# Order of the first projections, how queries and keys are turned, the instruction order of the first stage, and the PSUM banks of a hybrid encoder step

## The chip, the cores and the metric

The kernel runs on one core of a Trainium2 chip. The metric is the device time of one execution in microseconds. One execution is taken by the hardware profiler; its trace gives, for each engine, when each instruction started, how long it took and what it waited for. TensorE (PE) multiplies matrices into PSUM, a memory of eight banks; VectorE (DVE) and ScalarE (ACT) read PSUM and work elementwise; GpSimd (POOL) does small elementwise work; SyncE (SP) issues nearly all transfers (DMAs).

## What is computed

One layer of a streaming encoder, for 256 prompt frames and 8 streams of 16 new frames each: 384 rows (three blocks of 128) of width 2048.

```python
h = rmsnorm(x, norm_mix_g)
proj = h @ w_in                      # columns: GLU pair | q | k | v | forget logits | gate A | gate B
u = glu_in[..., :D_CONV] * sigmoid(glu_in[..., D_CONV:])
z = layernorm(causal_dwconv(concat(conv_buf, u), conv_dw_w, conv_dw_b), conv_ln_g, conv_ln_b)
a_out = (z * sigmoid(z)) @ conv_pw_out
q, k = rmsnorm(q, q_norm_g), rmsnorm(k, k_norm_g)        # per head of 128
logf = log_sigmoid(f_logit + b_forget)
b_out = attn(q, k, v, logf) @ w_att_out                  # 8 heads, bias = cumulative logf, causal
x = x + (gate_a * a_out + gate_b * b_out) @ w_out
up = rmsnorm(x, norm_ffn_g) @ w_up                       # 2 x 5632 columns
x = x + (silu(causal_dwconv(g_half)) * u_half) @ w_down
```

The sample streams also attend to 128 cached keys and values each. Besides `x`, the new keys, values, log forget gates and convolution states are returned. All is float32.

## The kernel before

**Matmuls.** Each weight is read once. `planned` (line 155) lists the weight tiles in the order in which they are used; a unit is two 128-row blocks of one column group. `ahead` (199) fetches units by `fetch` (132, SP's queue, three buffers `raw`) and calls `split` (148): ScalarE copies the unit into a rounded high part `hi` (line 145) and VectorE computes the rest `lo` (146). Activations are kept as such a pair too. A product is then three matmuls (lines 244 to 246, or 239 to 241 in the transposed kind): high with high, high with low, low with high. `gemm` (221) runs a list of jobs; a job is one group of up to 512 columns over all 16 blocks of rows, with one PSUM bank for each of the three row blocks. The tiles come from two pools: `acc` with five banks and `misc` with three. All three of a job come from `acc`, but for the second job of a pair, whose third comes from `misc`. After the last block the job's `evac` moves the banks to SBUF.

**Side work.** After every block of rows (an iteration) `gemm` calls `tick`, which advances generators given to it; through them small steps are placed between matmuls. TensorE's instructions are issued in program order. On the other engines a scheduler chooses the order by priority and by its own estimate of when data will be there. Two means fix it: `tc.high_priority(offset=...)`, and `queued` (92), which chains an instruction behind the one on its engine that was queued last. Before, `queued` is used for transfers on SP alone.

**The first stage.** `x_chunk(c)` (282) turns a 128-column chunk of x on TensorE (285) and ScalarE (288) and VectorE (289) make its high and low part `hT`. Chunks 0 and 1 and the first two units are made in a prologue, the others by `first_norm` (388) during the first gemm (439): the value columns are three groups of 344 (the last one with the eight forget logits), the first two as a pair, the third alone. Chunks 2 and 3 are made in iterations 3 and 4. `first_norm` also squares x on ScalarE (400) and computes the row scale `rs1`, which the evacuations `tok_evac` (423) apply. Then come the forget logits, the value outputs (465, 466), the keys (514, with `bias_rows` beside), scaling of the keys by their norm (519, 520) and the key outputs, the queries (524) and their scaling (528).

**Attention and GLU.** The GLU projection (745) has four jobs with four banks each; its 64 iterations carry `attention` (651) and the depthwise convolution `conv` (686) as side work. Head h starts at iteration 5 + 6h: `head_past_keys` (569) turns cached keys on VectorE, `head_operands` (576) turns the head's query and key on TensorE (lines 583 and 587, three transposes each) and copies them out of PSUM (584 ScalarE, 588 VectorE), `head_scores` (592), `head_probs` (617), `head_out` (629) and `head_last` (646) follow at offsets 2, 4, 9, 11 and 13. `load_k` and `load_v` (546, 553) fetch caches and bias rows for a head, through SP.

**Later stages.** Gates (823), attention and convolution outputs (834, 874), the output projection (932) and the feed-forward part (1027) are `gemm` calls of the same kind. `blocks` (255) turns a panel of 384 x 512 by 16 VectorE transposes of 32 x 384; it is used there already (line 259). `mix_panel` (857) is such a use, and `mix_chunk` (847) turns the last panel on TensorE.

Of the kernel before, what the change touches and what calls it, by code (L numbers as in the profile page):

```python
# [19 lines left out]
H = 8  # L20
# [13 lines left out]
SPLIT_AHEAD, EVAC_AHEAD = 150, 400  # L34
# [6 lines left out]
def hybrid_step(  # L41
# [66 lines left out]
    make_identity(nc, ident[:])  # L108

    def newton_rsqrt(r, s, m):  # L110
        nc.scalar.activation(s, m, AF.Sqrt)
# [79 lines left out]
    v_last = len(plan) - 16  # L191
    ready = []
# [28 lines left out]
    def gemm(jobs, sides=()):  # L221
        for js in jobs:
            js = js if isinstance(js, tuple) else (js,)
            for j in js:
                nb = 4 if j["kind"] == "A" else NTT
                j["ps"] = [(misc_tile if j is not js[0] and i == 2 else acc_tile)() for i in range(nb)]
            for j, k in [(j, k + i) for k in range(0, js[0]["nk"], 2) for j in js for i in range(2)]:
# [19 lines left out]
                if sp:  # L247
                    with tc.high_priority(offset=EVAC_AHEAD):
                        for m in range(nb):
                            j["evac"](m, ps[m])  # L250
                    if "done" in j:
# [30 lines left out]
    def x_chunk(c):  # L282
# [5 lines left out]
        nc.scalar.activation(hi, ps[:, :NT], AF.Identity, scale=g)  # L288
        stt(lo, ps[:, :NT], g, f(hi), op0=ALU.mult, op1=ALU.subtract)  # L289
# [57 lines left out]
    for v, r, n in rows:  # L347
        nc.gpsimd.dma_start(vrow[r:r + n, :], v[0].rearrange("(c p) -> c p", p=P))
    kg = p_qkv.tile([P, P], F32, name="kg")
    nc.gpsimd.dma_start(kg[:], k_norm_g[0].partition_broadcast(P))  # L350
    bf = p_qkv.tile([P, H], F32, name="bf")
    nc.gpsimd.dma_start(bf[:], b_forget[0].partition_broadcast(P))
# [35 lines left out]
    def first_norm():  # L388
        for c in range(2, 16, 2):
# [6 lines left out]
            if c % 4 == 2:  # L396
                for t in range(NTT):
                    n = c // 4
                    tc.keep_in_program_order(
                        nc.scalar.activation(junk[:], xs[n][:, t, :], AF.Square, accum_out=ssx[:, t, n:n + 1]))  # L400
            yield
            if c > 2:
                yield
        mt = p_x0.tile([P, NTT], F32, name="mt")
        nc.vector.tensor_reduce(mt[:], ssx[:], axis=mybir.AxisListType.X, op=ALU.add)
        ts(mt[:], mt[:], 1.0 / DM, EPS, op0=ALU.mult, op1=ALU.add)
        r = rsqrt(mt[:], [P, NTT], p_x0, "r1")
        nc.vector.tensor_copy(rs1[:], r[:])
        for _ in range(12):
# [13 lines left out]
    def tok_evac(dst, c0, n, sq=None, shared=True):  # L423
        def ev(t, ps):
            if shared and t % 2:
                ts(dst[:, t, c0:c0 + n], ps[:, :n], rs1[:, t:t + 1], None, op0=ALU.mult)
            else:
                nc.scalar.activation(dst[:, t, c0:c0 + n], ps[:, :n], AF.Identity, scale=rs1[:, t:t + 1])
            if sq is not None:
                for i in range(n // P):  # L430
                    jk = p_qkv.tile([P, P], F32, tag="jk", bufs=2, name="jk")
                    h = c0 // P + i
                    nc.scalar.activation(jk[:], dst[:, t, h * P:(h + 1) * P], AF.Square,
                                         accum_out=ssq[:, sq, t, h:h + 1])
# [4 lines left out]
    gemm([(v_jobs[0], v_jobs[1]), v_jobs[2]], [first_norm()])  # L439
    close_x0()  # L440
# [23 lines left out]

    nc.sync.dma_start(prompt_v[0, 0].rearrange("(t p) h d -> p t (h d)", p=P), vt[:, 0:2, 0:1024])
    nc.sync.dma_start(sample_v[0].rearrange("b t h d -> (b t) (h d)"), vt[:, 2, 0:1024])
# [47 lines left out]
    gemm([job("B", 16, ha, tok_evac(kt, 512 * i, 512, 0)) for i in range(2)], [bias_rows()])  # L514
    close_b()
    rk = head_rsqrt(0)
# [6 lines left out]

    gemm([job("B", 16, ha, tok_evac(qt, 512 * i, 512, 1)) for i in range(2)])
    rq = head_rsqrt(1)
    for t in range(NTT):
        q3 = qt[:, t, :].rearrange("p (h d) -> p h d", h=H)
        tt(q3, q3, rq[:, t, :].unsqueeze(2).to_broadcast([P, H, P]), op=ALU.mult)
# [15 lines left out]
    kcs, vbs = {}, {}  # L544
# [8 lines left out]
    def load_v(h):  # L553
        vc = p_att.tile([P, 8, P], F32, tag="vc", bufs=2, name="vc")
        nc.sync.dma_start(vc[:], cache_v[0, :, :, h, :].rearrange("b p d -> p b d"))
        bs = p_att.tile([P, 5 * P], F32, tag="bs", bufs=2, name="bs")
# [8 lines left out]
        vbs[h] = vc, bs  # L565
# [10 lines left out]
    def head_operands(d):  # L576
        hs = d["hs"]
        d["vc"], d["bs"] = vbs[d["h"]]
        qT = p_att.tile([P, NT], F32, tag="qT", bufs=2, name="qT")
        kT = p_att.tile([P, NT], F32, tag="kT", bufs=2, name="kT")  # L580
        ps = misc_tile()
        for t in range(NTT):
            tr(ps[:, t * P:(t + 1) * P], qt[:, t, hs], ident[:])
        nc.scalar.activation(qT[:], ps[:, :NT], AF.Identity, scale=qgs[:])
        ps = misc_tile()
        for t in range(NTT):
            tr(ps[:, t * P:(t + 1) * P], kt[:, t, hs], ident[:])
        nc.vector.tensor_copy(kT[:], ps[:, :NT])
        nc.vector.tensor_copy(qz[d["h"] % 2][:, :, :, 0:16], by_stream(qT[:, 2 * P:]))
        d["qT"], d["kT"] = qT, kT  # L590

    def head_scores(d):
        qT, kT, kTs, bs, qzh = d["qT"], d["kT"], d["kTs"], d["bs"], qz[d["h"] % 2]
# [479 lines left out]
```

## Time and profile before

| | us |
|---|---|
| median of three runs | 2005.61 |
| lowest and highest run | 2002.94, 2005.78 |
| the profiled execution | 2005.83 |
| its span in the trace | 2003.9 |
| TensorE busy | 1992.6 |
| VectorE busy | 1272.2 |
| ScalarE busy | 742.1 |

The span runs from the first to the last instruction. Busy time of TensorE is modelled, since matmuls overlap in its pipeline: two matmuls that start 0.22 us apart are each shown with 0.39 us. So distances between starts tell more than durations. The granted clock is the share of TensorE's full clock, 2.4 GHz; its other level is 1.2 GHz.

### The profile page before, as it was taken

How to read it: one execution, taken by the hardware profiler on the slowest of the kernel's cores; microseconds unless marked ns; L12 is line 12 of the kernel's file. 1: busy time of each engine (PE TensorE's matmuls, PEld its weight loads, DVE VectorE, ACT ScalarE, POOL GpSimd, SP SyncE). 2: the span in 40 equal slices, each digit the busy share in tenths (PEclk: the TensorE clock that was granted, in tenths of full speed). 3: DMA queues.
4: the chain of work that ended last, by engine and by line, in shares of the span. 5: the costliest groups of instructions: out<-in, count | busy, mean ns of one | idle time of the engine just before them, and what ended most of it. 6: DMA issues, size and time to landing. Idle time of an engine off the chain costs nothing.

```text
span 2003.9 us, 24493 instructions
## 1 busy us (share of the span) xinstructions
PE 1992.6 (99%) x9431; PEld 1681.5 (84%) x9431; DVE 1272.2 (63%) x1852; ACT 742.1 (37%) x1077; POOL 87.2 (4%) x216
## 2 busy tenths in 40 slices
PE   8999999999999999999999999999999999999999
PEld 8988999988888887888888888888888888888887
DVE  4435478888765487676867683367673376638663
ACT  5434455433334523334433432233332233323321
POOL 2000001100000000000010000001000000000000
PEclk9999999999999999999999999999999999999999
DMA  6566566444444334534444444444443444344443
GB/s 179 176 175 175 137 163 167 120 140 131 132 134 125 127 121 142 185 121 133 127 137 116 137 127 137 126 127 126 129 135 127 133 120 137 126 129 125 137 157 106
DMA packets 209254, 275.99 MB, mean 138 GB/s; under 512 B 55878, under 2 KB 96729, under 8 KB 209129
## 3 DMA queue, kind: packets, MB, share of 16 engines
q1 hardware_dynamic: 208817, 273.85, 46.3%
q8 instruction: 74, 1.21, 0.2%
q0 software_dynamic: 288, 0.57, 0.2%
q14 instruction: 43, 0.35, 0.1%
q10 hardware_dynamic: 32, 0.01, 0.0%
HBM read 266.98 MB, written 7.86 MB: 137 GB/s over the span
## 4 chain that ended last, share of the span: by engine, by line
PE 95%; DVE 4%; issue 1%; DMA 1%; ACT 0%; SPq 0%; ACTq 0%; DVEq 0%
PE acc L244 28%; PE acc L246 28%; PE acc L245 28%; PE acc L239 2%; PE acc L241 2%; PE acc L240 2%; DVE mixT L259 1%; DVE lo L146 1%; DMA raw<-in_w_in_dram 1%; DVE sgA L843 0%; DVE uT L259 0%; DVE sgA L844 0%; PE misc L636 0%; PE misc L603 0%; PE misc L285 0%
## 5 line engine op out<-in xcount | busy, mean ns | idle before, releaser
L146 DVE TENSOR_TENSOR lo<-raw,hi 128x1024 fp32r<-128x1024 f32 (+2 forms) x481 | 579.6, 1205 | 582.7 <-ACT hi L145 579.0
L145 ACT CAST hi<-raw 128x1024 fp32r<-128x1024 f32 (+2 forms) x481 | 496.0, 1032 | 994.2 <-PE acc L246 869.1
L244 PE MATMUL acc<-hi,xg 128*128 128x512 f32 x1056 | 411.8, 390 | 0.0
L246 PE MATMUL acc<-hi,xg 128*128 128x512 f32 x1056 | 410.9, 389 | 0.0
L245 PE MATMUL acc<-lo,xg 128*128 128x512 f32 x1056 | 410.8, 389 | 0.0
L244 PE MATMUL acc<-hi,hT 128*128 128x512 f32 (+1 forms) x704 | 268.5, 381 | 2.4 <-ACT hT L288 2.4
L246 PE MATMUL acc<-hi,hT 128*128 128x512 f32 (+1 forms) x704 | 266.0, 378 | 0.4 <-DVE hT L289 0.4
L245 PE MATMUL acc<-lo,hT 128*128 128x512 f32 (+1 forms) x704 | 265.8, 377 | 0.0
L244 PEld LDWEIGHTS acc<-hi,xg 128*128 128x128 f32 x1056 | 198.2, 188 | 42.3
L246 PEld LDWEIGHTS acc<-hi,xg 128*128 128x128 f32 x1056 | 198.2, 188 | 41.3
L245 PEld LDWEIGHTS acc<-lo,xg 128*128 128x128 f32 x1056 | 198.2, 188 | 40.6
L244 PE MATMUL acc<-hi,act 128*128 128x512 f32 x528 | 205.5, 389 | 0.5 <-DVE y L1018 0.5
L246 PE MATMUL acc<-hi,act 128*128 128x512 f32 x528 | 205.4, 389 | 0.0
L245 PE MATMUL acc<-lo,act 128*128 128x512 f32 x528 | 205.4, 389 | 0.0
L722 DVE SCALAR_TENSOR_TENSOR ut<-ext,cw,ut 128x384 f32<-128x384 f32 x240 | 151.5, 631 | 6.1
L244 PEld LDWEIGHTS acc<-hi,hT 128*128 128x128 f32 x704 | 132.7, 189 | 25.3 <-ACT hT L288 2.7
L246 PEld LDWEIGHTS acc<-hi,hT 128*128 128x128 f32 x704 | 132.7, 189 | 23.3 <-DVE hT L289 0.7
L245 PEld LDWEIGHTS acc<-lo,hT 128*128 128x128 f32 x704 | 132.8, 189 | 22.2
L259 DVE STREAM_TRANSPOSE extf<-tok 32x384 f32<-32x384 f32 x176 | 100.3, 570 | 30.9 <-ACT tok L954 28.2
L259 DVE STREAM_TRANSPOSE uT<-tok 32x384 f32<-32x384 f32 x176 | 100.3, 570 | 29.7 <-ACT tok L954 26.9
L244 PEld LDWEIGHTS acc<-hi,act 128*128 128x128 f32 x528 | 99.1, 188 | 21.6 <-DVE y L1018 0.9
L245 PEld LDWEIGHTS acc<-lo,act 128*128 128x128 f32 x528 | 99.1, 188 | 20.5
(289 smaller groups left out, 2079.7 us busy)
## 6 DMA issues: line engine op xcount, KB each, us to landing
raw<-in_w_up_dram SPq DMA_DIRECT2D x176, 512.0 KB
raw<-in_w_in_dram SPq DMA_DIRECT2D x96, 512.0 KB
raw<-in_w_down_dram SPq DMA_DIRECT2D x88, 512.0 KB
raw<-in_w_in_dram SPq DMA_DIRECT2D x64, 256.0 KB
raw<-in_w_out_dram SPq DMA_DIRECT2D x32, 512.0 KB
raw<-in_w_att_out_dram SPq DMA_DIRECT2D x16, 512.0 KB
raw<-in_conv_pw_out_dram SPq DMA_DIRECT2D x16, 512.0 KB
raw<-in_w_in_dram SPq DMA_DIRECT2D x23, 344.0 KB
```

The costliest lines, as they stand in the source:

```text
L145: nc.scalar.copy(hi[:, k, :o], raw[:, k, :o])
L146: tt(lo[:, k, :o], raw[:, k, :o], f(hi[:, k, :o]), op=ALU.subtract)
L239: mm(o, hi[:, kk, s], ah, start=st, stop=False)
L240: mm(o, hi[:, kk, s], al, start=False, stop=False)
L241: mm(o, lo[:, kk, s], ah, start=False, stop=sp)
L244: mm(o, ah[:, s], hi[:, kk, :n], start=st, stop=False)
L245: mm(o, ah[:, s], lo[:, kk, :n], start=False, stop=False)
L246: mm(o, al[:, s], hi[:, kk, :n], start=False, stop=sp)
L259: nc.vector.transpose(put(a, slice(32 * b, 32 * b + 32)), src[32 * a:32 * a + 32, b])
L722: stt(o, v, wc, o, op0=ALU.mult, op1=ALU.add)
```

## The change

The change has four parts, and they touch the first 20% of the kernel and the choice of banks in all of it.

- **Order.** The first pair is the first and third value group; then come the queries, the keys, and the second value group alone; then the GLU as before. The value outputs move behind the second value group. `first_norm` spreads over the first gemm and the query gemm, and its pool is closed after that.
- **Queries and keys.** `q_panel` and `k_panel` turn them with `blocks` on VectorE, four heads at a time: queries during the key gemm (at iterations 2 and 12) into `attT`, which ScalarE scales in place; keys during the second value group (at 3 and 13) into the memory of the queries. `head_operands` keeps the cached keys and one small copy. Squares for the norms are issued after a job's evacuation, not within it.
- **First stage chained.** `queued` now also chains, while the first pair and four more units are fetched, the splits, the two parts of each x chunk, the last squares, the root and the ScalarE evacuations, in program order; on GpSimd the identity stands ahead of the small loads. Attention steps get a priority of 250. Bias rows are loaded apart from the cached values, which are loaded one head ahead; the last two steps of a head move by one iteration.
- **Banks.** With `wide=True` the third bank of every job comes from `misc`, so that five and three banks rotate; this is set for every gemm but the first, the second value group and the GLU.

```diff
     ident = cp.tile([P, P], F32, name="ident")
-    make_identity(nc, ident[:])
+    nc.gpsimd.memset(ident[:], 0.0)
+    queued(nc.gpsimd.affine_select(out=ident[:], in_=ident[:], pattern=[[-1, P]], compare_op=ALU.not_equal, fill=1.0,
+                                   base=0, channel_multiplier=1))
...
-        nc.scalar.copy(hi[:, k, :o], raw[:, k, :o])
-        tt(lo[:, k, :o], raw[:, k, :o], f(hi[:, k, :o]), op=ALU.subtract)
+        first = in_first()
+        queued(nc.scalar.copy(hi[:, k, :o], raw[:, k, :o]), first)
+        queued(tt(lo[:, k, :o], raw[:, k, :o], f(hi[:, k, :o]), op=ALU.subtract), first)
...
-    planned(w_in, 0, V_COLS[0], 16, V_COLS[1])
-    for cols in V_COLS[2:] + K_COLS + Q_COLS + GLU_COLS + GA_COLS + GB_COLS:
+    planned(w_in, 0, V_COLS[0], 16, V_COLS[2])
+    for cols in Q_COLS + K_COLS + V_COLS[1:2] + GLU_COLS + GA_COLS + GB_COLS:
...
+    def in_first():
+        return len(plan) >= v_last - 4
...
-                j["ps"] = [(misc_tile if j is not js[0] and i == 2 else acc_tile)() for i in range(nb)]
+                j["ps"] = [(misc_tile if i == 2 and (wide or j is not js[0]) else acc_tile)() for i in range(nb)]
...
-        nc.scalar.activation(hi, ps[:, :NT], AF.Identity, scale=g)
-        stt(lo, ps[:, :NT], g, f(hi), op0=ALU.mult, op1=ALU.subtract)
+        with tc.high_priority(offset=EVAC_AHEAD):
+            queued(nc.scalar.activation(hi, ps[:, :NT], AF.Identity, scale=g))
+            queued(stt(lo, ps[:, :NT], g, f(hi), op0=ALU.mult, op1=ALU.subtract))
...
-    gemm([(v_jobs[0], v_jobs[1]), v_jobs[2]], [first_norm()])
-    close_x0()
+    norm_steps = first_norm()
+    gemm([(v_jobs[0], v_jobs[2])], [norm_steps])
...
+    gemm([tok_job(qt, 512 * i, 512, 1) for i in range(2)], [norm_steps, bias_rows()], wide=True)
+    drain(norm_steps)
...
+    def q_panel(n):
+        blocks(qt[:, :, 512 * n:512 * (n + 1)], by_feature(attT[:, 4 * n:4 * n + 4]))
+        for h in range(4 * n, 4 * n + 4):
+            nc.scalar.activation(attT[:, h], attT[:, h], AF.Identity, scale=qgs[:])
+
+    kT = qt[:].rearrange("p t n -> p (t n)").rearrange("p (h x) -> p h x", h=H)
+
+    def k_panel(n):
+        blocks(kt[:, :, 512 * n:512 * (n + 1)], by_feature(kT[:, 4 * n:4 * n + 4]))
+
+    for n in range(2):
+        after(2 + 10 * n, lambda n=n: q_panel(n))
+    gemm([tok_job(kt, 512 * i, 512, 0) for i in range(2)], wide=True)
...
+    for n in range(2):
+        after(3 + 10 * n, lambda n=n: k_panel(n))
+    gemm([v_jobs[1]])
+    nc.sync.dma_start(prompt_v[0, 0].rearrange("(t p) h d -> p t (h d)", p=P), vt[:, 0:2, 0:1024])
+    nc.sync.dma_start(sample_v[0].rearrange("b t h d -> (b t) (h d)"), vt[:, 2, 0:1024])
...
     def head_operands(d):
-        hs = d["hs"]
-        d["vc"], d["bs"] = vbs[d["h"]]
-        qT = p_att.tile([P, NT], F32, tag="qT", bufs=2, name="qT")
-        kT = p_att.tile([P, NT], F32, tag="kT", bufs=2, name="kT")
-        ps = misc_tile()
-        for t in range(NTT):
-            tr(ps[:, t * P:(t + 1) * P], qt[:, t, hs], ident[:])
-        nc.scalar.activation(qT[:], ps[:, :NT], AF.Identity, scale=qgs[:])
-        ps = misc_tile()
-        for t in range(NTT):
-            tr(ps[:, t * P:(t + 1) * P], kt[:, t, hs], ident[:])
-        nc.vector.tensor_copy(kT[:], ps[:, :NT])
-        nc.vector.tensor_copy(qz[d["h"] % 2][:, :, :, 0:16], by_stream(qT[:, 2 * P:]))
-        d["qT"], d["kT"] = qT, kT
+        head_past_keys(d)
+        d["bs"] = bss[d["h"]]
+        nc.vector.tensor_copy(qz[d["h"] % 2][:, :, :, 0:16], by_stream(attT[:, d["h"], 2 * P:]))
...
-            for off, step in ((0, head_past_keys), (2, head_operands), (4, head_scores), (9, head_probs),
-                              (11, head_out), (13, head_last)):
+            for off, step in ((1, head_operands), (4, head_scores), (9, head_probs),
+                              (12, head_out), (14, head_last)):
```

## Rows read from the trace of the kernel before

**Rows 1.** The page's first part: busy us of each engine, share, instructions.

```profile
PE 1992.6 (99%) x9431; PEld 1681.5 (84%) x9431; DVE 1272.2 (63%) x1852; ACT 742.1 (37%) x1077; POOL 87.2 (4%) x216
```

**Rows 2.** Busy time by stretch: stretch, PE, PEld, DVE, ACT, POOL (starts); clock, DMA share, GB/s.

```profile
75.00:100.00 25.00, 25.00 (x135) 22.50 (x134) 12.10 (x28) 9.93 (x12) 0.00 (x0) 1.00 0.75 230
...
175.00:200.00 25.00, 25.00 (x112) 20.71 (x111) 8.62 (x8) 10.97 (x32) 0.00 (x0) 1.00 0.61 171
...
225.00:250.00 25.00, 25.00 (x161) 24.57 (x160) 14.74 (x31) 9.72 (x17) 0.81 (x2) 1.00 0.62 158
...
275.00:300.00 25.00, 25.00 (x191) 23.85 (x190) 24.07 (x57) 11.77 (x24) 1.16 (x2) 1.00 0.71 167
...
1700.00:1725.00 25.00, 24.52 (x108) 19.96 (x108) 20.57 (x31) 9.78 (x13) 0.00 (x0) 1.00 0.40 133
```

**Rows 3.** Timeline at 12.8 to 17.8 us: start, duration, what [idle before it <- releaser].

```profile
12.85 0.77 ACT L145 CAST hi<-raw 128x688 fp32r<-128x688 f32 x1 [3.96 <-DMA raw<-in_w_in_dram]
...
14.94 0.77 ACT L145 CAST hi<-raw 128x688 fp32r<-128x688 f32 x1 [1.32 <-DMA raw<-in_w_in_dram]
15.61 0.57 ACT L288 ACTIVATE hT<-misc,gm 128x384 fp32r<-128x384 f32 x1
...
16.23 0.43 PE L244 MATMUL acc<-hi,hT 128*128 128x344 f32 x1 [2.44 <-ACT hT L288]
...
16.53 0.61 DVE L289 SCALAR_TENSOR_TENSOR hT<-misc,gm,hT 128x384 fp32r<-128x384 f32 x1
...
17.19 0.45 PE L246 MATMUL acc<-hi,hT 128*128 128x344 f32 x1 [0.38 <-DVE hT L289]
```

**Rows 4.** Busy time by slices of 2 us behind that pause, columns as in rows 2.

```profile
16.00:18.00 2.00, 1.39 (x5) 1.11 (x6) 2.00 (x4) 1.97 (x6) 0.00 (x0) 0.86 0.64 181
18.00:20.00 2.00, 2.00 (x8) 2.00 (x8) 0.45 (x1) 1.41 (x4) 0.00 (x0) 0.50 0.95 305
20.00:22.00 2.00, 2.00 (x12) 1.98 (x12) 0.00 (x0) 0.44 (x1) 0.00 (x0) 0.78 0.68 223
```

**Rows 5.** Timeline of PE around the transposes of one head.

```profile
249.77 0.34 PE L241 MATMUL acc<-hT,lo 128*128 128x384 f32 x1
249.95 0.49 PE L583 MATMUL misc<-ident,qt 128*128 128x128 f32 x3
...
250.52 0.42 PE L239 MATMUL acc<-hT,hi 128*128 128x384 f32 x1
250.78 0.33 PE L240 MATMUL acc<-hT,hi 128*128 128x384 f32 x1
```

**Rows 6.** Groups by line and shape, DVE and ACT: busy us, mean ns of one.

```profile
L259 DVE STREAM_TRANSPOSE yT<-y 32x384 f32<-32x384 f32 x64 | 36.5, 570 | 1.2
...
L146 DVE TENSOR_TENSOR lo<-raw,hi 128x688 fp32r<-128x688 f32 x23 | 20.2, 878 | 35.2 <-ACT hi L145 35.0
...
L519 DVE TENSOR_TENSOR kt<-kt,rq0r 128x1024 f32<-128x1024 f32 x3 | 3.6, 1220 | 0.0
...
L433 ACT ACTIVATE jk<-kt 128x128 f32<-128x128 f32 x24 | 7.1, 298 | 0.1
```

**Rows 7.** Timeline of PE where a job waits for a bank or operand.

```profile
721.59 0.39 PE L246 MATMUL acc<-hi,zt 128*128 128x512 f32 x1
722.16 0.50 PE L244 MATMUL acc<-hi,zt 128*128 128x512 f32 x1 [0.18 <-DVE sgB L828]
722.50 0.40 PE L245 MATMUL acc<-lo,zt 128*128 128x512 f32 x1
...
755.32 0.50 PE L244 MATMUL acc<-hi,zt 128*128 128x512 f32 x1 [0.19 <-DVE sgB L828]
...
791.91 0.33 PE L850 MATMUL misc<-ident,sgA 128*128 128x128 f32 x1 [0.23 <-DVE sgA L844]
...
1721.80 0.39 PE L246 MATMUL acc<-hi,act 128*128 128x512 f32 x1
1722.67 0.50 PE L244 MATMUL acc<-hi,act 128*128 128x512 f32 x1 [0.48 <-DVE y L1018]
```

More of the change, by code (lines that the diff above doesn't have):

```diff
@@ L219, in tick, with gemm @@
             next(g, None)
-    def gemm(jobs, sides=()):
+    def gemm(jobs, sides=(), wide=False):
         for js in jobs:
@@ L398, in first_norm @@
                     n = c // 4
[L399 to L402, printed above, removed]
+                    sq = nc.scalar.activation(junk[:], xs[n][:, t, :], AF.Square, accum_out=ssx[:, t, n:n + 1])
+                    if c == 14:
+                        queued(sq)
+                    else:
+                        tc.keep_in_program_order(sq)
+            if c < 14:
+                yield
+            if 2 < c < 14:
                 yield
         mt = p_x0.tile([P, NTT], F32, name="mt")
[L405 to L409, printed above, removed]
+        with tc.high_priority(offset=EVAC_AHEAD):
+            nc.vector.tensor_reduce(mt[:], ssx[:], axis=mybir.AxisListType.X, op=ALU.add)
+            ts(mt[:], mt[:], 1.0 / DM, EPS, op0=ALU.mult, op1=ALU.add)
+            r = rsqrt(mt[:], [P, NTT], p_x0, "r1")
+            nc.vector.tensor_copy(rs1[:], r[:])
+        for _ in range(14):
             yield
@@ L421, in hybrid_step, with tok_job, post, tok_evac @@
     ssq = p_qkv.tile([P, 2, NTT, H], F32, name="ssq")
-    def tok_evac(dst, c0, n, sq=None, shared=True):
+    def tok_job(dst, c0, n, sq):
+        d = job("B", 16, ha, tok_evac(dst, c0, n))
+        def post():
+            for t in range(NTT):
+                for h in range(c0 // P, (c0 + n) // P):
+                    jk = p_qkv.tile([P, P], F32, tag="jk", bufs=2, name="jk")
+                    nc.scalar.activation(jk[:], dst[:, t, h * P:(h + 1) * P], AF.Square,
+                                         accum_out=ssq[:, sq, t, h:h + 1])
+        d["post"] = post
+        return d
+    def tok_evac(dst, c0, n, shared=True):
         def ev(t, ps):
@@ L427, in ev @@
             else:
[L428 to L434, printed above, removed]
+                queued(nc.scalar.activation(dst[:, t, c0:c0 + n], ps[:, :n], AF.Identity, scale=rs1[:, t:t + 1]),
+                       in_first())
         return ev
@@ L659, in attention @@
                 step, d = at[t]
-                step(d)
-                if step is head_out and d["h"] + 2 < H:
-                    load_v(d["h"] + 2)
+                with tc.high_priority(offset=ATT_AHEAD):
+                    step(d)
+                if step is head_probs and d["h"] + 2 < H:
+                    load_b(d["h"] + 2)
+                if step is head_probs and 0 < d["h"] < H - 1:
+                    load_v(d["h"] + 1)
             yield
@@ L741, in hybrid_step @@
     load_k(0)
+    load_b(0)
     load_v(0)
+    load_b(1)
     load_v(1)
@@ L822, in hybrid_step @@
     ln_steps = conv_branch()
-    gemm([job("B", 16, ha, sig_evac(sg, n)) for sg in (sgA, sgB) for n in range(4)], [ln_steps])
+    gemm([job("B", 16, ha, sig_evac(sg, n)) for sg in (sgA, sgB) for n in range(4)], [ln_steps], wide=True)
     def ao_evac(n):
@@ L832, in ao_job @@
         return job("B", 8, grouped(aHL), ao_evac(n))
-    gemm([ao_job(n) for _, n in AO_PW[:2]], [ln_steps])
+    gemm([ao_job(n) for _, n in AO_PW[:2]], [ln_steps], wide=True)
     drain(ln_steps)
@@ L874, in hybrid_step @@
     gemm([ao_job(n) if what == "ao" else job("B", 8, grouped(zt), pw_evac(n), done=pw_done(n))
-          for what, n in AO_PW[2:]])
+          for what, n in AO_PW[2:]], wide=True)
     res = {}
@@ L930, in second_norm @@
         nc.vector.tensor_copy(rs2[:], r2[:])
-    gemm([job("B", 16, grouped(mix), wo_evac(n), done=wo_done(n)) for n in range(4)])
+    gemm([job("B", 16, grouped(mix), wo_evac(n), done=wo_done(n)) for n in range(4)], wide=True)
     p_f, y, xg, rs2, close_f, close_r = (res[k] for k in ("f", "y", "xg", "rs2", "close_f", "close_r"))
@@ L1026, in hybrid_step @@
     for what, g in FFN_PLAN:
-        gemm(up_jobs(g) if what == "up" else down_jobs(g, g[-1] == 10))
+        gemm(up_jobs(g) if what == "up" else down_jobs(g, g[-1] == 10), wide=True)
     pe_order.__exit__(None, None, None)
```

41 lines of the change are left out of this document (21 added, 20 removed).

## The prediction

> **What bounds the kernel now.** I read the page's busy shares first: TensorE is busy for 99% of the span [rows 1]. A share of 99% says that the time is the sum of what TensorE is given, so an edit pays in three ways only: it takes instructions off TensorE, it ends one of TensorE's few pauses, or it avoids matmuls at the low clock. Next I read the busy times by stretch [rows 2]. In 175 to 200 us 112 full matmuls start, so one takes 25.00/112 = 0.223 us, and TensorE is full in every stretch shown but the last, even where VectorE is itself nearly full (24.07 of 25.00 us in 275 to 300) or where the 1.5 MiB of values go out (75 to 100). VectorE has 8.62 us of work in 175 to 200. Last I looked for TensorE's pauses: one at 14 us [rows 3], followed by a stretch at the lower clock [rows 4], and a few of under half a microsecond where the next accumulation waits for a bank [rows 7].
>
> **The change part by part.** The sum is made against the profiled execution, 2005.83 us for a span of 2003.9; the median of the runs, 2005.61, is 0.2 us from it, which I neglect.
>
> *Queries and keys turned by VectorE.* Before, `head_operands` turns the three 128-row blocks of a head's query and of its key on TensorE. The first of six transposes starts at 249.95, the next main matmul at 250.52, that is 0.57 us; and this matmul holds the next one off until 250.78, 0.26 us where such matmuls lie 0.18 apart (249.77 to 249.95) [rows 5]. So 0.57 + 0.08 = 0.65 us a head, and 8 heads give 5.2 us. These lie on TensorE, on the path, and go entirely. VectorE instead gets `blocks`: 16 transposes for each panel of four heads, two panels for queries and two for keys, 64 in all. The nearest row is the same form elsewhere, 0.570 us [rows 6], so 36.5 us, less the eight copies `kT<-PSUM` that fall away. They lie beside the key projection and the last value block. The first has room: the two panels of queries are 18.3 us, and the key gemm is 288 matmuls of 0.223, 64 us, in which VectorE's other work is about a third by the stretch 175 to 200. For keys the room is narrower and is the second rival. Price here: 0 as long as that cover holds. Below nothing is possible only through the small copies; I leave it at 0.
>
> *First stage chained.* The pause at 14 us: ScalarE takes the third weight unit at 12.85, when it lands, then waits for the fourth, which lands at 14.94, and only then, at 15.61, evacuates chunk 2 of x, whose transposes TensorE had finished at 13.8 (16.23 less the 2.44 that it then stood). The main matmuls resume at 16.23 and, after a second wait for VectorE's half, at 17.19 [rows 3]. In the chain the order is that of the program: the split of unit 3 is issued before the third iteration, chunk 2 and chunk 3 behind it, and unit 4 after them. So chunk 2's high half starts when the split ends, 12.85 + 0.77 = 13.62, and ends 0.57 later at 14.2; its low half follows the split's low half on VectorE (13.6 + 0.88 [rows 6] = 14.5) and ends 0.61 later, at 15.1. The third matmul can then start at 15.1 instead of 17.19: a gain of 2.05 us, which the landing at 12.85 does not let grow. Unit 4 has landed by 14.94 and is needed only an iteration pair later, near 17.7; nothing new is late behind it at once. The squares of the norm stand in that gap and might delay it by some 0.5 us.
>
> Behind the pause comes a stretch at 1.2 GHz: the granted clock is 0.86, 0.50 and 0.78 in the three slices of 2 us from 16 to 22 [rows 4], so 2 x (0.14 + 0.50 + 0.22) = 1.7 us of full-clock work are lost. Whether this goes too is not shown: the new pauses, about 0.4 us at 13.8 and 0.6 before the third matmul, lie between one of 2.44 us that was followed by the low clock [rows 3] and one of 0.48 us that was not (clock 1.00 in 1700 to 1725 [rows 2, 7]). Bounds 0 and 1.7; they are nearer to the short one in size, so I take 1.7. The identity made ahead of the small loads starts the warm-up earlier, but the third unit's landing at 12.85 sets what follows, so I count at most 0.2 us and take 0.
>
> The chain also puts the last squares, the root and the splits in one line on ScalarE. Evacuations of the first value block need that root. It was ready in time before, with the same work ahead of it and only one wider split now between, so I take 0; bound 1 us of loss.
>
> *Order of the blocks.* The matmuls of values, queries and keys are the same in number and width; only their order changes, so 0 on TensorE. What moves with them: the two output DMAs of the values (1.5 MiB), from the stretch 75 to 100 to behind the last value block, at about 215 us, past the caches' loads on SP's queue; the key outputs, also 1.5 MiB, are issued during that block. Behind them on SP stand weight loads. The cover is the three raw buffers and three split ones; the third rival is that it is gone. The later value cache loads (at the step before use, not two heads ahead) have 9 iterations of 12 matmuls, about 19 us, before they are read: 0.
>
> *Eight banks.* `wide` puts the third accumulation of each job into the other pool, so a job no longer waits for the one before it to be evacuated. At 722 the start-to-start distance is 0.57 us and the next one, 0.34, is 0.11 over the pitch, so 0.57 - 0.23 + 0.11 = 0.46; a second such wait is at 755; at 1722 it is 0.87 - 0.23 + 0.11 = 0.75 [rows 7]. Together 1.7 us. A fourth of this kind, at the first job of the output projection, I count at 0: at 791.91 TensorE waits anyway for VectorE's `sgA`, and VectorE does not get there sooner. The pool keeps one or two banks for the small transposes, where a wait may appear; with the boundary from the last value block, whose three evacuations are all ScalarE's, I take 0.5 us of loss, with bounds 0 and 2.
>
> Sum: 5.2 + 2.05 + 1.7 + 1.7 - 0.5 = 10.15 us, so 2005.8 - 10.15 = 1995.7.
>
> **The rivals.** *The pause keeps its clock, or more.* The low clock stays after the shorter pauses: 1.7 us less, 1997.4. If the third unit's transfer and not ScalarE's order holds the stage, so that the chain does not do what it says, its 3.75 us go altogether: 1999.4. Against that speaks that the transposes were done at 13.8 and only ScalarE stood between.
>
> *VectorE becomes the bound between the values and the gates.* From the start of the last value block the keys need 12 squares on ScalarE, 0.30 us each with a read behind each, 4 to 7 us in all, then the root and six multiplications of 1.22 us, 32 transposes of 0.57 and the splits, 0.88 each [rows 6]: with the root the first panel is ready at about 8 + 7.3 + 9.1 and 8 for nine splits, 32 us, both at about 32 + 9.1 and another 8 for splits and evacuations, 50. The first scores stand at the tenth iteration of the gate stage, about 16 x 9 matmuls of 344 columns, 0.15 us each by the pitch of 512, and 9 iterations of 12 x 0.18: 21.6 + 19.4 = 41 us. So there are 9 us to spare if the panels run in order. If the first waits for the second, TensorE stands for 9 us, and its clock may fall: 2005.8 - 10.15 + 9 = 2004.7, near no change; half of it gives 2000.2. For it: VectorE has 24.07 us of work in 275 to 300. Against: 14.74 in 225 to 250 [rows 2], where the panels spill. The Trainium skill, "VectorE: DVE Perf Modes", section "Rules for kernel authors", says to turn a 128x128 block on TensorE when PSUM will do as its destination, which speaks against this edit; by it the cost is VectorE's 36 us against TensorE's 5, and the result would be this rival's. The trace has TensorE full and VectorE at 63%, so the cheaper engine is the dearer one here.
>
> *Outputs ahead of weights.* Key and value outputs, 3.1 MB, are issued within some 10 us near 215 us; at the 230 GB/s of 75 to 100 [rows 2] they take 13.7 us. Weight loads behind them on the queue are late by that, less some 8 us of weights already split (three units of 2.7 us, 18 matmuls of 0.15): if the cover is only that, 6 us are lost; if the buffers are empty because the block of 344 columns eats them as fast as they come, 13.7 and a low clock of 1.7, and the kernel ends at 2005.8 - 10.15 + 15.4 = 2011, slower than before. It decides from 10 us of starvation on. Against it: the values alone went out in 75 to 100 and TensorE was busy for 25.00 of 25.00 us.
>
> **How the numbers follow.** Forecast, with its small terms, 1993 to 1997: 0.52. Low clock stays: 0.18, 1997.4. Chain without effect: 0.09, 1999.4. VectorE bound: 0.12, 2000 to 2004.7, half on either side of 2001.6. Outputs ahead of weights: 0.09, of which 0.05 slower than before by over 4 us and 0.02 each between and below. A difference of 0.2%, 4 us, is about what a measurement of this kernel can tell. So faster 0.52 + 0.18 + 0.09 + 0.06 + 0.02 = 0.87, which I lower to 0.85 for what is not listed; same 0.09; slower 0.06. The range goes from 1992.9 (the sum without its 0.5, with the 0.2 of the start, and 2 us of spread between runs) to 2001.5, where the middle of the VectorE case lies; about 0.15 is left out above, a little below.
>
> **What would show it.** No `misc<-ident,qt` and `kt` on TensorE, and 64 more transposes of 0.57 on VectorE, on tiles of keys and queries. In the first 25 us TensorE's wait for `hT` under 0.6 us, third matmul of the third unit near 15.1, granted clock 1.00 in 18 to 22; a 0.50 there is the first rival. No wait on `sgB` or `y` at a job's start. A wait of the scores' line on a key tile shows the second rival, a wait of the splits for their DMA between 210 and 250 us the third. The forecast is wrong if TensorE's summed idle time does not fall.

## The result and the profile after

The changed kernel takes 2009.2 us (median of 17 runs, 2006.7 to 2010.59) beside 2005.35 for the kernel before (17 runs, 2002.94 to 2007.56): a ratio of 1.002 with a 95% interval of [1.0012, 1.0027]. It is slower by about 4 us, where 1995.7 was forecast and the range ended at 2001.5. The profiled execution took 2009.34 us.

The page of the kernel after, span and busy times of the engines:

```profile
span 2007.4 us, 24443 instructions
PE 1988.3 (99%) x9383; PEld 1677.0 (84%) x9383; DVE 1306.7 (65%) x1908; ACT 742.6 (37%) x1077; POOL 85.4 (4%) x216
```

Beside [rows 1], TensorE has 48 instructions fewer (six transposes for each of 8 heads) and 4.3 us less to do, VectorE 56 more (64 transposes less eight copies). That is the change as described. But TensorE's idle time, span less busy, rose from 2003.9 - 1992.6 = 11.3 us to 2007.4 - 1988.3 = 19.1. The prediction named that as the sign that it is wrong. What TensorE waited for, in the kernel after (engine and line, what it waited for: us in total, times, longest us):

```profile
PE misc L740 <- DVE mx L638: 9.1, 1, 9.1
PE misc L661 <- DVE mx L638: 2.0, 1, 2.0
...
PE acc L250 <- ACT hT L297: 0.2, 1, 0.2
```

The waits that were to go are gone: 2.44 us for the first stage's `hT` [rows 3] is 0.2, and no job waits for `sgB` or `y` [rows 7]. The first two lines are new, 11.1 us together. They wait for VectorE's line 638, which adds the bias rows to a head's scores. A table by stage, each stage counted from TensorE's first matmul of it, shows that they eat more than everything that was gained (us, worked out from the starts in TensorE's timelines):

| kernel | start to GLU | GLU projection with attention | sigmoid gates to the end | span |
|---|---|---|---|---|
| before | 218.46 | 171.59 | 1613.83 | 2003.9 |
| after | 214.41 | 180.98 | 1612.02 | 2007.4 |
| difference | -4.05 | +9.39 | -1.81 | +3.5 |

So the question is what happened between 214 and 395 us. The chain, read backwards in the kernel after. First the matmul that TensorE stood for 9.10 us before (timeline of PE: start, duration, line, tiles, idle time before it and its releaser):

```profile
267.13 0.38 PE L628 MATMUL misc<-qt,attT 128*128 128x128 f32 x2
...
277.19 0.48 PE L740 MATMUL misc<-ident,ut 128*128 128x128 f32 x1 [9.10 <-DVE mx L638]
```

TensorE issued head 2's scores at 267.13 and then had nothing to go on with: its next instruction needs a `misc` bank, and the three that it has just filled are emptied by VectorE's line 638. VectorE, in turn (timeline of DVE):

```profile
268.16 1.25 DVE L611 STREAM_TRANSPOSE kTs<-kc 128x1024 f32<-128x1024 f32 x1 [3.31 <-PE misc L632]
269.33 0.18 DVE L619 COPY qz<-attT 128x128 f32<-128x128 f32 x1
...
276.84 0.29 DVE L638 CUSTOM_DVE_ANT_0 pr<-misc,bs 128x128 f32<-128x128 f32 x1 [5.06 <-POOL bs L603]
```

waited 5.06 us for GpSimd, which masks head 2's bias rows; GpSimd had not got them before 276.08 (timeline of POOL; this row names no releaser, the next rows of line 603 name the bias rows' DMA):

```profile
276.08 0.72 POOL L603 TENSOR_TENSOR bs<-bs,mk 128x256 f32<-128x256 f32 x1 [23.67 <-issue]
```

And the rows were late because SP issued three of their four transfers only from 271.63 on (timeline of SP's queue, kernel after; `bs` are bias rows, `kc` cached keys, `raw` weights):

```profile
240.72 0.41 SPq L597 DMA_DIRECT2D bs<-c_dr  x1
241.22 3.85 SPq L587 DMA_DIRECT2D kc<-in_cache_k_dram  x4
245.18 1.31 SPq L139 DMA_DIRECT2D raw<-in_w_in_dram  x2
253.36 3.68 SPq L587 DMA_DIRECT2D kc<-in_cache_k_dram  x4
257.14 3.07 SPq L139 DMA_DIRECT2D raw<-in_w_in_dram  x6
269.43 2.15 SPq L587 DMA_DIRECT2D kc<-in_cache_k_dram  x4
271.63 0.65 SPq L598 DMA_DIRECT2D bs<-c_dr  x1
...
272.80 0.61 SPq L600 DMA_DIRECT2D bs<-d_dr  x1
```

After the first bias row come three sets of cached keys, and between 257.14 + 3.07 = 260.21 and 269.43 SP issues nothing at all. The waits of SP in that kernel say why:

```profile
SPq L587 <- DVE qz L619: 13.4, 2, 9.2
SPq L587 <- DVE mx L640: 7.1, 2, 6.8
```

The third set stands 9.2 us for a `kc` buffer. There are two, and each set starts when a head's transposition of cached keys (line 611) has ended: 253.36 behind one from 252.09 to 253.33, 269.43 behind the one from 268.16 to 269.41. That last one is head 3's, so the load at the front of SP's queue is head 5's; the rows behind it are those of head 2, which is two whole heads nearer. The view of SP's waits names the VectorE instruction that ended last (619, 640); by their starts the sets follow line 611, which reads the buffer. Head 3's transposition needs the tile `kTs` that head 2's scores were reading until TensorE had issued them at 267. So a transfer that VectorE reads only at 314.44 (head 5's transposition) waited for TensorE's own progress, with the one that TensorE needed next behind it.

The second wait, 2.00 us before 335.46, has another last link. Head 5's rows were late on the queue too (three of their four transfers from 321.62 on, behind two sets of keys), but GpSimd had masked them by 328.06. VectorE reached line 638 only at 335.12, after other work that it did without a pause (timelines of POOL and DVE; line 754 belongs to the convolution):

```profile
327.29 0.77 POOL L604 TENSOR_TENSOR bs<-bs,mk 128x128 f32<-128x128 f32 x1
...
330.96 2.57 DVE L754 SCALAR_TENSOR_TENSOR ut<-ext,cw,ut 128x384 f32<-128x384 f32 x4
...
335.12 0.28 DVE L638 CUSTOM_DVE_ANT_0 pr<-misc,bs 128x128 f32<-128x128 f32 x1
```

Both waits go when the key loads alone are moved (e1 below), so the order of the loads stands behind this one too. Whether it did so through the order chosen for VectorE, or through work that the first wait had put off, is not shown.

In the kernel before, the order on the queue around the same time (timeline of SP):

```profile
243.51 0.41 SPq L557 DMA_DIRECT2D bs<-c_dr  x1
...
244.91 0.61 SPq L560 DMA_DIRECT2D bs<-d_dr  x1
245.62 0.40 SPq L550 DMA_DIRECT2D kc<-in_cache_k_dram  x1
```

What turned it round is in the diff: the attention steps run under `tc.high_priority(offset=ATT_AHEAD)`, and `head_past_keys`, part of the step, issues `load_k` (line 614), so these loads got the priority; `load_b` and `load_v` (692, 694) stand behind the `with` block and did not.

The price is the waits and the clock behind them (kernel after, stretches of 5 us; columns as in rows 2, the clock third from last):

```profile
270.00:275.00 5.00, 0.00 (x0) 0.00 (x0) 1.78 (x2) 0.00 (x0) 0.00 (x0) 0.60 1.02 145
275.00:280.00 5.00, 2.81 (x10) 2.75 (x11) 3.16 (x16) 2.42 (x10) 1.13 (x2) 0.50 0.84 269
280.00:285.00 5.00, 5.00 (x41) 4.68 (x40) 4.75 (x8) 1.51 (x3) 1.64 (x2) 0.87 0.61 179
...
335.00:340.00 5.00, 4.54 (x31) 4.00 (x32) 4.96 (x20) 2.81 (x9) 0.00 (x0) 0.66 0.76 168
```

Full-clock work lost behind the first wait is 2.81 x 0.50 + 5.00 x 0.13 = 2.1 us, behind the second (before 335.46) 4.54 x 0.34 = 1.5. With 11.1 of waits that is 14.7 us; the stage without these waits, in the experiment e5 below, is 180.98 - 166.10 = 14.9 shorter.

### The profile page after: what moved, and what is told of

Read it like the earlier page. It is cut to its first block, busy times and chain, and to the rows that moved or that the text cites. A ratio compares the mean times of both kernels' runs of the same rounds, so it can differ in the third digit from the quotient of the medians.

```text
span 2007.4 us, 24443 instructions
## 1 busy us (share of the span) xinstructions
PE 1988.3 (99%) x9383; PEld 1677.0 (84%) x9383; DVE 1306.7 (65%) x1908; ACT 742.6 (37%) x1077; POOL 85.4 (4%) x216
## 4 chain that ended last, share of the span: by engine, by line
PE 96%; DVE 2%; issue 1%; DMA 0%; SPq 0%; ACT 0%; POOL 0%; DVEq 0%; ACTq 0%
PE acc L250 20%; PE acc L252 20%; PE acc L251 20%; PE misc L250 10%; PE misc L251 10%; PE misc L252 10%; PE acc L245 2%; PE acc L246 2%; PE acc L247 2%; DVE lo L149 0%; DVE mixT L267 0%; DMA raw<-in_w_in_dram 0%; DVE ut L754 0%; PE misc L665 0%; PE misc L293 0%
## 5 line engine op out<-in xcount | busy, mean ns | idle before, releaser
L250 PE MATMUL acc<-hi,xg 128*128 128x512 f32 x704 | 274.9, 390 | 0.0
L252 PE MATMUL acc<-hi,xg 128*128 128x512 f32 x704 | 273.9, 389 | 0.0
L251 PE MATMUL acc<-lo,xg 128*128 128x512 f32 x704 | 273.9, 389 | 0.0
L250 PE MATMUL acc<-hi,hT 128*128 128x512 f32 (+1 forms) x512 | 193.0, 377 | 0.2 <-ACT hT L297 0.2
L251 PE MATMUL acc<-lo,hT 128*128 128x512 f32 (+1 forms) x512 | 190.4, 372 | 0.5 <-DVE lo L149 0.5
L252 PE MATMUL acc<-hi,hT 128*128 128x512 f32 (+1 forms) x512 | 190.5, 372 | 0.2
L250 PEld LDWEIGHTS acc<-hi,xg 128*128 128x128 f32 x704 | 132.1, 188 | 28.4
L252 PEld LDWEIGHTS acc<-hi,xg 128*128 128x128 f32 x704 | 132.1, 188 | 27.5
L252 PE MATMUL misc<-hi,xg 128*128 128x512 f32 x352 | 137.0, 389 | 0.0
L250 PE MATMUL misc<-hi,xg 128*128 128x512 f32 x352 | 137.0, 389 | 0.0
L251 PE MATMUL misc<-lo,xg 128*128 128x512 f32 x352 | 136.9, 389 | 0.0
L250 PE MATMUL acc<-hi,act 128*128 128x512 f32 x352 | 136.9, 389 | 0.0
L251 PE MATMUL acc<-lo,act 128*128 128x512 f32 x352 | 136.9, 389 | 0.0
L252 PE MATMUL acc<-hi,act 128*128 128x512 f32 x352 | 136.9, 389 | 0.0
L252 PEld LDWEIGHTS acc<-hi,hT 128*128 128x128 f32 x512 | 96.1, 188 | 16.0 <-DVE hT L298 0.7
```

The source lines that it names most:

```text
L250: mm(o, ah[:, s], hi[:, kk, :n], start=st, stop=False)
L251: mm(o, ah[:, s], lo[:, kk, :n], start=False, stop=False)
L252: mm(o, al[:, s], hi[:, kk, :n], start=False, stop=sp)
```

## The experiments

The theory: the priority put the loads of cached keys ahead of the bias rows on SP's queue, which goes in order. The rivals were the prediction's: VectorE short of time between the values and the gates, or the transfers short of bandwidth behind the outputs, and a third, that the arithmetic under the priority (not its loads) pushes VectorE's other work back. Ratios are to the kernel before on the same chip (2005.16, 2004.13 and 2005.38 us for the three groups e1 to e4, e5 to e8, e9 and e10); comparisons across groups go by the ratios.

**e1: the key loads without the priority, all else as in the change.**

```diff
     def head_past_keys(d):
...
-        if d["h"] + 1 < H:
-            load_k(d["h"] + 1)
...
                 with tc.high_priority(offset=ATT_AHEAD):
                     step(d)
+                if step is head_operands and d["h"] + 1 < H:
+                    load_k(d["h"] + 1)
```

> The changed kernel, with one edit: the cached keys of the next head are loaded after the step and outside its priority, so that on SP's queue they no longer overtake the bias rows. Theory (bias rows of a head stand on the queue behind key loads that wait for a buffer): TensorE's 9.1 and 2.0 us waits for the scores' VectorE step disappear, and with them some 3 us of low clock, so about 2009.3 - 14.5 = 1995. Rival A (the value and key outputs, moved next to the gate stage, fill the transfer engines, so the rows land late in any order): 2007 to 2010, waits still there. Rival B (VectorE's panels for keys make it late): 2007 to 2010 as well.

Measured 1998.38 us, 0.9964 [0.9951, 0.9977]. The GLU stage fell from 180.98 to 170.25, and both waits for line 638 are gone; on SP the four bias rows go out together at 240.94 to 242.34 and the keys behind them. The time is 3.4 us above the expected 1995. One smaller wait is left, for a head's turned keys (waits of TensorE, e1):

```profile
PE misc L630 <- DVE kTs L611: 2.5, 1, 2.5
```

These keys were issued from 336.87 to 340.08; VectorE turned them at 351.66, behind a weight split for whose high part it had stood 1.13 us, so here it is VectorE's order that made TensorE wait.

VectorE's work and the bandwidth were left as they were, so neither rival explains the 11 us.

**e2: the other way round, the bias rows get the priority too.**

```diff
-                    load_b(d["h"] + 2)
+                    with tc.high_priority(offset=ATT_AHEAD):
+                        load_b(d["h"] + 2)
```

> The changed kernel, with the bias rows' loads given the same priority as the steps, the key loads left as they are. Theory: the four loads of a head's bias rows stand together again on the queue and ahead of the key loads, 1995 to 1997. Rivals A and B: 2007 to 2010.

Measured 2015.33 us, 1.005 [1.0033, 1.0067]: a miss, and in the wrong direction. The wait for the bias rows did go, but now the bias rows themselves stand at the front of the queue for their own buffer (waits of SP, e2):

```profile
SPq L597 <- DVE mx L638: 23.6, 4, 8.4
SPq L597 <- DVE mx L640: 12.0, 1, 12.0
```

and what stands behind them is late instead, the weights above all (waits of TensorE, e2; lines 245 and 247 are matmuls of the GLU projection):

```profile
PE acc L245 <- ACT hi L148: 6.1, 2, 4.3
PE acc L247 <- DVE lo L149: 3.5, 3, 1.9
PE misc L665 <- DMA vc<-in_cache_v_dram: 3.0, 1, 3.0
```

I had expected that it mattered which of two loads comes first. It matters that a load whose buffer is not free is at the front at all: whatever is behind pays. That is a correction of my theory, and e9 tries it.

**e3: the key loads keep the priority but have a third buffer.**

```diff
-        kc = ... tag="kc", bufs=2, name="kc")
+        kc = ... tag="kc", bufs=3, name="kc")
```

> The changed kernel with three buffers for cached keys in place of two, priorities as they are: the key loads still stand ahead of the bias rows, but have a buffer to go to. Theory that it is the wait of the load in front, and not its place alone: the 9.1 us wait goes or falls under 2 us, 1994 to 2000. If the place in the queue and the bytes in front alone count: still 5 us or more of waits, 2003 to 2009. Rivals A and B: 2007 to 2010.

Measured 2001.67 us, 0.9985 [0.9976, 0.9994], some 7 us better than the change itself (1.002) and a little above what was expected. The 9.1 us wait is 2.2, the 2.0 became 2.5 (waits of TensorE, e3):

```profile
PE misc L661 <- DVE mx L638: 2.5, 1, 2.5
PE misc L740 <- DVE mx L638: 2.2, 1, 2.2
```

The rows were there for both. VectorE came to line 638 late, behind a weight split for whose high part it had stood 2.73 and 3.17 us; why that part was late was not looked into. So the load that waits for its buffer is about half of the cost (7 of the 13.6 us between the change and e5 below), and the rest stays with the order.

**e4: the kernel before, with the priority alone.** Its attention steps, in which `load_k` is issued too, are wrapped as in the change; nothing else is touched.

```diff
-                step(d)
+                with tc.high_priority(offset=250):
+                    step(d)
```

> The kernel before with one edit: its attention steps, with the key loads within them, get the priority of 250; nothing else of the change. Theory: the same waits arise there, since the key loads overtake the bias rows, 2009 to 2025. Rivals A and B, in which the moved outputs or the panels are needed for the loss: 2004 to 2007.

Measured 2029.66 us, 1.0121 [1.0106, 1.0136]: 24 us slower, more than the upper end of what was expected. The same two waits, larger (waits of TensorE; lines of the kernel before, where 609 adds the bias):

```profile
PE misc L709 <- DVE mx L609: 14.2, 1, 14.2
PE misc L632 <- DVE mx L609: 6.5, 1, 6.5
```

and on SP the bias rows have moved from 243.51 to 279.71, behind key loads (timeline of SP, e4):

```profile
274.94 2.44 SPq L550 DMA_DIRECT2D kc<-in_cache_k_dram  x4
...
279.71 0.53 SPq L557 DMA_DIRECT2D bs<-c_dr  x1
```

The second wait is again one with the rows there: masked by 343.90, read by line 609 at 350.91. None of the new order of the blocks, the turns on VectorE or the moved outputs is in this kernel. So they aren't needed for the loss; the priority is enough.

**e5: the change with the queue put right.** Key loads as in e1 but two heads ahead and into three buffers, so that no load stands for a buffer.

```diff
-        kc = ... tag="kc", bufs=2, name="kc")
+        kc = ... tag="kc", bufs=3, name="kc")
...
-        if d["h"] + 1 < H:
-            load_k(d["h"] + 1)
...
                     step(d)
+                if step is head_operands and d["h"] + 2 < H:
+                    load_k(d["h"] + 2)
...
     load_v(1)
+    load_k(1)
```

> The changed kernel with the key loads out of the priority, three buffers for cached keys, and each head's key load issued two heads ahead, so that no load on SP's queue waits for a buffer that is still in use. Theory: no wait of TensorE on the scores' operands is left, the gate stage takes 171.6 - 5.2 = 166.4 us, and the time is the forecast of the sum, 1994 to 1996. If something else in the change costs time there (VectorE's panels, the moved outputs): 1998 or more, as in the run with the key load alone moved.

Measured 1994.67 us (1993.46 to 1995.22), 0.9952 [0.9938, 0.9965], faster than both kernels. All that TensorE waits for by 0.2 us or more (waits of TensorE, e5):

```profile
PE misc L317 <- POOL ident L109: 1.5, 1, 1.5
PE misc L885 <- DVE sgA L879: 0.5, 2, 0.3
PE misc L521 <- ACT crow L515: 0.2, 1, 0.2
```

No wait in the GLU stage is left, and SP stands for no `kc` or `bs` buffer. The stage takes 166.10 us, 5.49 less than before. e6 to e8 each take one part of the change out of e5, which prices the other terms of the sum without the disturbance of the queue.

**e6: e5 without the rotation of eight banks.**

```diff
-                j["ps"] = [(misc_tile if i == 2 and (wide or j is not js[0]) else acc_tile)() ...
+                j["ps"] = [(misc_tile if i == 2 and j is not js[0] else acc_tile)() ...
```

> The same kernel as the one with key loads two ahead, with the third bank of a job taken from the five again, except for the pair. Price of the eight banks by the sum: 1.7 us slower than that run, nearly all behind the gate stage, with the three waits back. Rival, that the pauses only move: within 0.5 us of it.

Measured 1995.75 us, 0.9957 [0.9945, 0.997], 1.1 more than e5 by the medians. The last part, sigmoid gates to the end, is the cleaner reading: 1613.85 against 1612.07, 1.8 us. The three waits of [rows 7] are back (waits of TensorE, e6):

```profile
PE acc L250 <- DVE y L1053: 0.5, 1, 0.5
PE acc L250 <- DVE sgB L863: 0.4, 2, 0.2
```

**e7: e5 without the chain on ScalarE, VectorE and GpSimd** (SP's is kept, as before).

```diff
-        if chain and e in newest:
+        if chain and e in newest and e == ENG.SP:
```

> The same kernel as the one with key loads two ahead, with the chain on SP alone, so that ScalarE, VectorE and GpSimd are ordered by the scheduler in the first stage. Price by the sum: the 2.4 us pause at 14 us and the low clock behind it come back, 3 to 4 us slower than that run. Rival, that the landing of the third unit sets the stage: within 1 us.

Measured 1996.48 us, 0.9966 [0.9953, 0.9978]: 1.8 more than e5 by the medians, 2.8 in the time to the GLU (216.20 against 213.40), less than the 3 to 4 that I had expected. The pause is back, but shorter than in [rows 3], and the clock stays full behind it, where it fell to 0.50 in [rows 4] (timeline of PE, then windows of 2 us, e7):

```profile
15.84 0.43 PE L250 MATMUL acc<-hi,hT 128*128 128x344 f32 x1 [1.63 <-ACT hT L297]
...
16.00:18.00 2.00, 1.63 (x9) 1.34 (x10) 2.00 (x4) 1.97 (x5) 0.00 (x0) 1.00 0.72 188
18.00:20.00 2.00, 2.00 (x16) 1.98 (x15) 0.05 (x1) 1.39 (x5) 0.00 (x0) 1.00 0.98 310
```

So this execution, 1996.43 us at a mean granted clock of 1.000, gives a price of the chain without the clock. Two of e7's five runs took 1998.09 and 1999.52 us, at 0.999 and 0.998: 3.4 and 4.9 above e5. They have no trace, so where their clock fell is not known. GpSimd's chain is out as well, and the identity is late again (2.5 us of wait, 1.5 in e5).

**e8: e5 with queries and keys turned on TensorE**, six transposes and two copies a head, as before.

```diff
-    for n in range(2):
-        after(2 + 10 * n, lambda n=n: q_panel(n))
-    for n in range(2):
-        after(3 + 10 * n, lambda n=n: k_panel(n))
...
+        ps = misc_tile()
+        for t in range(NTT):
+            tr(ps[:, t * P:(t + 1) * P], qt[:, t, hs], ident[:])
+        nc.scalar.activation(qT1[:], ps[:, :NT], AF.Identity, scale=qgs[:])
+        (the same for kt into kT1, copied by VectorE)
```

> The same kernel as the one with key loads two ahead, with queries and keys turned on TensorE head by head, as before the change, and no panels on VectorE. Price by the sum: 48 transposes with their gaps, 5.2 us slower than that run. Rival (the page's rule, VectorE dearer): no slower, or faster by up to 5 us.

Measured 1999.98 us, 0.9979 [0.997, 0.9988], 5.3 more than e5. The GLU stage takes 171.58 against 166.10, or 5.48. Between the two profiled executions lie 6.5 us; the rest, 1.1, is in the time to the GLU, where kernels with the same first stage differ by as much (see the first-stage pause below).

**e9: e2 with a third buffer for the bias rows and one for the keys**, to try the correction.

```diff
-        kc = ... tag="kc", bufs=2, name="kc")
+        kc = ... tag="kc", bufs=3, name="kc")
-        bs = ... tag="bs", bufs=2, name="bs")
+        bs = ... tag="bs", bufs=3, name="bs")
```

> The changed kernel with the bias rows' loads under the priority, as in the second run, and three buffers each for bias rows and cached keys. Theory (a load that waits for its buffer holds all loads behind it on SP's one queue): the waits of 23.6 and 12.0 us on SP for a free bias buffer go, weights are no longer late, and the 2015 of the second run falls to 1994 to 1998. Rival (the loads ahead of the weights cost by their bytes, not by their wait): 2008 to 2016.

Measured 2000.89 us, 0.998 [0.9971, 0.999]. Half a hit: 0.7% better than e2, and its waits for weights are gone, but it is above the expected range, with this wait of TensorE left:

```profile
PE misc L665 <- DMA vc<-in_cache_v_dram: 4.7, 1, 4.7
```

The bias rows still keep SP standing (17.1 us in four waits for their buffer), and now the cached values, which have no priority, are the ones behind. One buffer more moves the cost, it does not end it.

**e10: the change with `ATT_AHEAD` at 0**, that is, without any priority for the attention steps.

```diff
-SPLIT_AHEAD, ATT_AHEAD, EVAC_AHEAD = 150, 250, 400
+SPLIT_AHEAD, ATT_AHEAD, EVAC_AHEAD = 150, 0, 400
```

> The changed kernel with the attention steps' priority set to zero, for their arithmetic as well as for their loads; two key buffers. Theory: the load order alone made the loss, so the time is that of the run with the plain key load, 1997 to 1999.5, with one late load of keys left. Rival, that the priority of the arithmetic is needed to keep TensorE fed: 2001 or more, with waits on ScalarE's or VectorE's attention steps.

Measured 1998.37 us, 0.9965 [0.9953, 0.9977], the same as e1 and with the same one wait of 2.5 us for a head's turned keys. In e1 the steps' arithmetic keeps the priority and only the loads lose it. So the priority of the arithmetic neither costs nor brings anything that these runs can tell, and the third rival falls.

## Why the prediction was wrong, point by point

**The step that failed** is the paragraph "Order of the blocks". It priced what the change moves on SP's queue by when a load is read ("9 iterations of 12 matmuls, about 19 us, before they are read: 0") and gave a zero for the value loads, while the bias rows, which the change takes out of `load_v` and loads by themselves, and the key loads had no price at all. The priority of 250, which the description of the change names, appears nowhere in the sum. It should have been followed through every instruction that the step issues: one of them is `load_k`. Then [rows 7] would not have been the last place to look for waits; the question would have been what is queued behind a key load that waits for one of two buffers. The measured price of that step: 9.1 + 2.0 us of waits and 3.6 of low clock, 14.7, against a zero. The first wait is traced link by link to the queue; that the second belongs to the same step is shown by e1, not by its chain. By the medians, e5 against the change, 0.9952 against 1.002, is 0.68% or 13.6 us.

**Turns off TensorE: 5.2 us.** Held. e8 gives 5.3 by the medians and 5.48 in the stage. The 64 transposes on VectorE hide, as costed, at the duration of [rows 6] (groups by line and shape, kernel after; busy us, mean ns of one):

```profile
L267 DVE STREAM_TRANSPOSE attT<-qt 32x384 f32<-32x384 f32 x32 | 18.2, 570 | 0.5
L267 DVE STREAM_TRANSPOSE qt<-kt 32x384 f32<-32x384 f32 x32 | 18.2, 569 | 0.5
```

**First-stage pause: 2.05 us, and 1.7 of low clock.** The mechanism held in the kernel after; the size is less sure. The third matmul of the third unit, forecast at 15.1, started at 15.01 (timeline of PE, then windows of 2 us, kernel after):

```profile
14.05 0.43 PE L250 MATMUL acc<-hi,hT 128*128 128x344 f32 x1 [0.17 <-ACT hT L297]
...
15.01 0.43 PE L252 MATMUL acc<-hi,hT 128*128 128x344 f32 x1
...
18.00:20.00 2.00, 2.00 (x16) 1.98 (x15) 1.18 (x2) 1.31 (x3) 0.00 (x0) 1.00 0.81 265
```

The time to the GLU fell by 4.05 us, forecast 3.75. In the nine kernels with the chain it is 213.40 (e5) to 214.76 (e10), in the three without it 216.20 (e7), 217.86 (e4) and 218.46 (before): the chain's gain is clear of that spread, but it can be put only at 1.4 to 5.1 us. e7 prices chain and earlier identity together at 2.8, without the clock; the 1.3 that are left of 4.05 are within the spread. The 1.7 were read from one execution, and not every execution loses them: of the fifteen runs of the kernel before beside e5, nine took 2002.94 to 2004.42 us at a mean granted clock of 1.000, six 2004.49 to 2005.86 at 0.999. The first rival, low clock kept or chain without effect, occurred in none of the nine: their clock is 1.00 from 16 to 24 us.

**Eight banks: 1.7 us, less 0.5.** Held: 1.81 in the last part of the kernel, 1.8 by e6's stage, 1.1 by the medians. The small losses did not appear there.

**The rivals.** *VectorE as the bound* did not occur, though it was as full as feared: 24.61 of 25 us in the stretch from 200 to 225 (windows of 25 us, kernel after):

```profile
200.00:225.00 25.00, 25.00 (x157) 25.00 (x156) 24.61 (x34) 9.03 (x11) 0.00 (x0) 1.00 0.75 243
225.00:250.00 25.00, 25.00 (x160) 24.59 (x160) 19.77 (x39) 11.37 (x18) 0.00 (x0) 1.00 0.77 184
```

TensorE is full in both. In the second wait, at 335 us, VectorE was the last link, but with the convolution and not with the panels. The rule of the Trainium skill, "VectorE: DVE Perf Modes", section "Rules for kernel authors", is that a 128x128 block is turned on TensorE when PSUM will do. It states no price; read as one, as the prediction did, it would have had e8 ahead of e5. e8 is 5.3 us behind: here TensorE, busy for 99% of the span, is the engine with no time to spare.

*Outputs ahead of weights* had the right place, SP's queue, and a result near the one measured (2011 forecast for it, 2009.2 seen), but for another reason: outputs and weights together go by at 243 GB/s in 200 to 225 and TensorE stands for none of it. A time that fits is no evidence for the mechanism that gave it.

**The sum without the failed step.** The terms add up to 10.15 us. e5, which keeps all the parts of the change and repairs the queue, is 9.46 us below the kernel before on its chip (2004.13 against 1994.67). What was in the sum was right to 1 us by the medians; what was wrong was left out of it. Some of that closeness is luck: the profiled executions lie 12.3 us apart (2003.9 against 1991.6), and e6, e7 and e8 give the parts back as 1.1 + 1.8 + 5.3 = 8.2 by the medians.

**What stays open.** Why the scheduler puts the three bias rows of head 2 behind head 5's keys, but the first one ahead of them, was not looked into. Nor was the size of e4, whose GLU stage is 25.4 us longer than in the kernel before, where the change loses 14.9 against e5. The smaller waits that e1, e3 and e10 keep lie in the order of VectorE's instructions and not in a transfer that is seen to be late; how the place of a load moves that order was not followed.

## What to carry to other kernels

A priority given to a step goes to every transfer that the step issues, and on a queue that is served in order a transfer that waits for its buffer stops all those behind it, however urgent. So, before a step is moved or raised, list its DMAs, the buffer each will wait for and what is queued behind; issue loads outside the raised part, early enough and with a buffer that is already free. When TensorE's wait names an elementwise engine that was idle too, follow the chain on to the queue: here, for the first wait, it was four links long (TensorE, VectorE, GpSimd, SP), and only the last showed the cause.

## What the runs showed of the hardware that was not expected

The length of a pause did not tell what the clock did behind it. In the kernel after, the granted clock was 0.50 behind TensorE's pause of 9.10 us and 0.66 behind that of 2.00. In the first stage it fell to 0.50 behind 2.44 us in the kernel before [rows 3, 4] and behind 1.23 us in e4 (18 to 20 us), and stayed at 1.00 behind 1.63 us in e7. Behind pauses of 2.25 and 2.47 us in the GLU stage of e3 it was 1.00 too (265 to 320 us). Nor do all executions of one kernel agree: e3's ten runs go from 1999.94 us at a mean granted clock of 1.000 (the profiled one) to 2004.55 at 0.997. So the clock's share of a pause is a term with a range, and one profile gives one value out of it.

SP's time is not free: in the kernel after a set of four key loads keeps it for 2 to 4 us (3.85 at 241.22), beside 2.0 for the four transfers of a head's bias rows (275.55 to 277.55).
